# Five seven-product groups in every second gate-and-up block, gated results in DRAM, low parts on GpSimd

## The chip, the cores and the metric

The kernel runs on one core of a Trainium2 chip. The metric is device microseconds of one launch, the median of three timed runs. The engines are TensorE (PE in the profile; PEld is its weight load), VectorE (DVE), ScalarE (ACT), GpSimd (POOL) and SyncE (SP, which here only issues DMAs).

## The reference, cut to what matters

One decoder layer, 256 tokens, width 2048, all in float32: a first SwiGLU feed-forward network, a gated pair of token mixers (retention and sliding-window attention), a second SwiGLU network, and a gated input embedding, with a layer norm behind each.

```python
def swiglu(x, w_gu, w_down):
    g, u = jnp.split(x @ w_gu, 2, axis=-1)
    return (jax.nn.silu(g) * u) @ w_down

h = layer_norm(alpha * h + 0.5 * swiglu(h, w_ffn1_gu[i], w_ffn1_down[i]), ...)
mixed = (sigmoid(gate_r) * ret_branch + sigmoid(gate_a) * att_branch) @ w_mix_out[i]
h = layer_norm(alpha * h + mixed, ...)
h = layer_norm(alpha * h + 0.5 * swiglu(h, w_ffn2_gu[i], w_ffn2_down[i]), ...)
ple = jax.nn.sigmoid(h @ w_ple_gate[i]) * (p[i] @ w_ple_proj[i])
h = layer_norm(alpha * h + ple, ...)
```

`w_gu` is 2048 by 11264, `w_down` 5632 by 2048.

## The kernel before, in words

**Products.** A float32 product is made of three matmuls in the rounded type fp32r: the high part of each operand is a cast on ScalarE, the low part is VectorE's subtraction of the cast from the raw value, and TensorE adds high times high, high times low and low times high (`Sum.add`, L410 to L412). So each weight that arrives costs ScalarE a cast, VectorE a subtraction and TensorE its matmuls.

**Blocks and units.** The gate-and-up product of a feed-forward network ("f1", "f2") goes in 11 blocks (0 to 10), each of 512 gate and 512 up columns; a block walks through the 2048 rows in eight units of 256 rows and 1 MB of weights. A unit is of one of two kinds:

- A plain unit, "P" (class `Unit`): one cast of 128x2048 (tile `h...`), one subtraction of 128x2048 (tile `lo`, shown as `l...`), and 8 products, 24 matmuls of 128x512.
- A seven-product unit, "S" (class `Seven`): a 2x2 multiplication done with 7 products in place of 8, so 21 matmuls. VectorE makes four sums of the weights (tile `u`: 1024, 512 and 512 elements for each partition, L243, L247, L248), a low part of three weight blocks (`lb`, 1536, L253) and a low part of the sums (`lu`, 2048, L257); ScalarE casts the three blocks (`hb`) and the sums (`hu`, in two halves). The products `p1`, `p6`, `p7` and `q5` of all S units of a block are collected in four PSUM banks of their own (`f_gu7s` and the like for block 7), the others in the block's own four banks (`f1g`). In the last S unit of a block `p1` and `q5` come first, and `lu` is read by the sixth matmul.

An S unit also needs sums of the activations ("forms": `seven_forms`, four VectorE operations, a cast, a low part). They are made once for the units 0 to 3 in block 0 (tile `f1f`).

**A block's end.** After the last S unit `seven_common` copies `p1` to SBUF (ScalarE) and makes three VectorE sums out of PSUM into a tile `eve` (L499 to L501), which frees the four banks for the next block's `f1g`. After the last unit two more sums add the block's own banks (L831), ScalarE applies the silu, and VectorE multiplies (L836). TensorE transposes the result (`turned`, L789, eight 128x128 matmuls) in a later gap between two units, and ScalarE copies it to SBUF: tiles `f1a...`, 1 MB for two blocks, where they wait for the down product.

**The order.** ORDERS gives the units of each block: "PPSSPSSP" is units 4, 5, 0, 1, 6, 2, 3, 7, so four of eight are S. VectorE's order is set by two clocks that the program keeps while it is written out: `pump` hands VectorE weight work until its clock has come up to TensorE's, and `after` does so ahead of each sum from PSUM. SP loads the weights in the order of use, as far as the slots allow: SBUF holds 23 slots of 1 MB, and a call `weights(n)` says how many the weights may take. In the blocks 1 to 10 that number falls by one with every second block, as the `f1a` tiles fill up.

**Down product.** Two blocks over 44 row groups; `convert` makes the high and low part of the activations of a group (tiles `f1ac`), and the forms of four groups are made on the way (`sums`, `f1forms`). Between the two feed-forward networks stand the mixers, made of the same units. GpSimd does nothing after the constants are made.

## Time and profile before

| | |
|---|---|
| median of 3 runs | 2252.26 us (2251.83 to 2252.43) |
| the profiled execution | 2252.07 us, span 2250.2 us, 1.87 us around it |
| TensorE busy | 2242.8 us, 100% of the span, 10435 matmuls |
| VectorE busy | 2025.6 us, 90% |
| ScalarE busy | 1221.1 us, 54% |
| GpSimd busy | 0.7 us, 7 instructions |
| moved by DMA | 465.31 MB, 207 GB/s in the mean |

Gate-and-up blocks 2 to 10 of f1 follow each other every 41.69 us, the first of them from 91.41 us of the span. Numbers are lost in the profile's names: `lf_gu` is the low part of any P unit of such a block, `uf_gu`, `lbf_gu`, `luf_gu` are the tiles of any S unit. "Idle before" is the time that an engine stood still ahead of the instruction, and behind the arrow stands what ended it.

### The profile page before, as it was taken

To read this page: it belongs to the slowest core of one execution; us is meant where nothing else is said; L and a number is where in the kernel's file an instruction comes from. 1 tells how busy PE (TensorE), PEld (TensorE's weight loads), DVE (VectorE), ACT (ScalarE), POOL (GpSimd) and SP (SyncE) were. 2 spreads that over 40 slices of the span, in tenths; PEclk is the share of its full clock that TensorE was granted. 3 is DMA by queue.
4 is the path that set the end of the run, shared out by engine and by line. 5 is a ranking of instruction groups with operands and counts; after the bars stand their busy time and mean duration, and the time that the engine had idled before them with its cause. 6 is when DMAs were issued, how large, how long until landed. Compare 5 with 4: busy or idle time off the path is not lost.

```text
span 2250.2 us, 26572 instructions
## 1 busy us (share of the span) xinstructions
PE 2242.8 (100%) x10435; PEld 1870.6 (83%) x10435; DVE 2025.6 (90%) x1778; ACT 1221.1 (54%) x1030; POOL 0.7 (0%) x7
## 2 busy tenths in 40 slices
PE   9999999999999999999999999999999999999999
PEld 7888888888888888888888888888888888888887
DVE  7999999999997888899899878989999999989976
ACT  6655555555554455555555545455555566565542
POOL 0000000000000000000000000000000000000000
PEclk9999999999999999999999999999999999999999
DMA  8665665555577454355566665766566566555761
GB/s 318 206 214 179 214 206 186 190 204 206 210 271 264 166 221 150 137 197 193 168 210 220 195 215 195 271 230 216 174 206 213 185 201 207 187 213 214 281 268 70
DMA packets 189981, 465.31 MB, mean 207 GB/s; under 512 B 14368, under 2 KB 15904, under 8 KB 187296
## 3 DMA queue, kind: packets, MB, share of 16 engines
q1 hardware_dynamic: 188880, 462.43, 59.6%
q8 instruction: 82, 1.34, 0.2%
q10 hardware_dynamic: 976, 1.18, 0.2%
q14 instruction: 43, 0.35, 0.0%
HBM read 455.17 MB, written 8.39 MB: 206 GB/s over the span
## 4 chain that ended last, share of the span: by engine, by line
PE 99%; DMA 0%; DVE 0%; SPq 0%; ACT 0%; issue 0%; DVEq 0%; ACTq 0%
PE f1g L412 5%; PE f1g L410 5%; PE f1g L411 5%; PE f2g L411 4%; PE f2g L412 4%; PE f2g L410 4%; PE rqk L371 3%; PE aqk L371 2%; PE f2d L412 1%; PE f1d L411 1%; PE f2d L410 1%; PE f1d L410 1%; PE f1d L412 1%; PE f2d L411 1%; PE rqk L379 1%; PE f2e L412 1%
## 5 line engine op out<-in xcount | busy, mean ns | idle before, releaser
L208 DVE TENSOR_TENSOR lf_gu<-rf_gu,hf_gu 128x2048 fp32r<-128x2048 f32 x93 | 209.4, 2286 | 8.4 <-ACT hf_gu L204 8.4
L204 ACT CAST hf_gu<-rf_gu 128x2048 fp32r<-128x2048 f32 x93 | 175.9, 1909 | 34.4 <-DMA rf_gu<-in_f_gu 18.4
L257 DVE TENSOR_TENSOR luf_gu<-uf_gu,huf_gu 128x2048 fp32r<-128x2048 f32 x80 | 182.8, 2285 | 1.1 <-ACT huf_gu L249 1.1
L244 ACT CAST huf_gu<-uf_gu 128x1024 fp32r<-128x1024 f32 x80 | 84.2, 1053 | 141.8 <-DVE uf_gu L243 139.7
L412 PE MATMUL f1g<-lf_gu,xt 128*128 128x512 f32 x384 | 149.7, 390 | 0.5 <-DVE lf_gu L142 0.5
L410 PE MATMUL f1g<-hf_gu,xt 128*128 128x512 f32 x384 | 150.1, 391 | 0.1
L411 PE MATMUL f1g<-hf_gu,xt 128*128 128x512 f32 x384 | 149.7, 390 | 0.0
L208 DVE TENSOR_TENSOR lf_down<-rf_down,hf_down 128x2048 fp32r<-128x2048 f32 x60 | 136.2, 2287 | 13.5 <-ACT hf_down L204 5.5
L236 ACT CAST hbf_gu<-rf_gu 128x1536 fp32r<-128x1536 f32 x80 | 117.2, 1483 | 55.1 <-DMA rf_gu<-in_f_gu 40.2
L253 DVE TENSOR_TENSOR lbf_gu<-rf_gu,hbf_gu 128x1536 fp32r<-128x1536 f32 x80 | 140.1, 1751 | 0.0
L204 ACT CAST hf_down<-rf_down 128x2048 fp32r<-128x2048 f32 x60 | 114.3, 1913 | 47.5 <-DMA rf_down<-in_f_down 14.2
L410 PE MATMUL f2g<-hf_gu,ht 128*128 128x512 f32 x320 | 124.7, 390 | 0.0
L412 PE MATMUL f2g<-lf_gu,ht 128*128 128x512 f32 x320 | 124.7, 390 | 0.0
L411 PE MATMUL f2g<-hf_gu,ht 128*128 128x512 f32 x320 | 124.6, 390 | 0.0
L249 ACT CAST huf_gu<-uf_gu 128x1024 fp32r<-128x1024 f32 x80 | 84.2, 1052 | 34.2 <-DVE uf_gu L248 34.1
L243 DVE TENSOR_TENSOR uf_gu<-rf_gu 128x1024 f32<-128x1024 f32 x80 | 97.5, 1219 | 0.0
L412 PEld LDWEIGHTS f1g<-lf_gu,xt 128*128 128x128 f32 x384 | 72.1, 188 | 16.1 <-DVE lf_gu L142 1.2
L410 PEld LDWEIGHTS f1g<-hf_gu,xt 128*128 128x128 f32 x384 | 72.2, 188 | 15.3 <-ACT hf_gu L141 0.6
L411 PEld LDWEIGHTS f1g<-hf_gu,xt 128*128 128x128 f32 x384 | 72.3, 188 | 14.9
L257 DVE TENSOR_TENSOR luf_down<-uf_down,huf_down 128x2048 fp32r<-128x2048 f32 x28 | 64.0, 2287 | 7.8 <-ACT huf_down L249 5.9
L411 PEld LDWEIGHTS f2g<-hf_gu,ht 128*128 128x128 f32 x320 | 60.1, 188 | 12.4
L410 PEld LDWEIGHTS f2g<-hf_gu,ht 128*128 128x128 f32 x320 | 60.1, 188 | 12.4
(1331 smaller groups left out, 6418.6 us busy)
## 6 DMA issues: line engine op xcount, KB each, us to landing
rf_gu<-in_f_gu SPq DMA_DIRECT2D x350, 512.0 KB, 5.2
rf_down<-in_f_down SPq DMA_DIRECT2D x176, 512.0 KB, 4.5
rw_rv<-in_w_rv SPq DMA_DIRECT2D x32, 512.0 KB, 4.4
rrg<-in_w_in_f SPq DMA_DIRECT2D x32, 512.0 KB, 4.6
rgr<-in_w_in_f SPq DMA_DIRECT2D x32, 512.0 KB, 4.6
rw_ret<-in_w_ret SPq DMA_DIRECT2D x32, 512.0 KB, 5.0
rga<-in_w_in_f SPq DMA_DIRECT2D x32, 512.0 KB, 5.0
rw_mix<-in_w_mix SPq DMA_DIRECT2D x32, 512.0 KB, 4.5
```

Source lines behind the costliest of these rows:

```text
L204: act.copy(self.hi, self.raw)
L208: dve.tensor_tensor(self.lo, self.raw, self.hi, ALU.subtract)
L236: act.copy(quarters(self.hb), self.place.blocks(self.raw)[:, 1:])
L243: dve.tensor_tensor(at[:, 0:2], raw[:, 1:3], raw[:, 0:1].broadcast_to([P, 2, 2, 256]), ALU.add)
L244: act.copy(hu[:, 0:2], u[:, 0:2])
L249: act.copy(hu[:, 2:], u[:, 2:])
L253: dve.tensor_tensor(quarters(lb), raw[:, 1:], quarters(hb), ALU.subtract)
L257: dve.tensor_tensor(lu, u, hu, ALU.subtract)
L371: pe.matmul(ps[:, f], u.tile_of(kk)[0][:, f * P : (f + 1) * P], rhs(k), start=k == 0, stop=k == KD - 1,)
L410: pe.matmul(o, al, bh, start=first, stop=False)
L411: pe.matmul(o, ah, bh, start=False, stop=False)
L412: pe.matmul(o, ah, bl, start=False, stop=self.left == 0)
```

## The change

- Blocks 2, 4, 6 and 8 of both networks become "PSSPSSSP": units 5, 0, 1, 6, 2, 3, 4, 7 with five S. The fifth takes a second, smaller set of forms (`x4`), made in block 1 and held in a slot. In such a block no job is put between its units, so the transposes of the block before wait for the next block, which then has two sets.
- The gated results of two blocks are written to DRAM as soon as both are there (from ScalarE's queue, 1 MB, five times in a network), and are read back by SP (tiles `f1b...`) during the last block and the first down block. Weights may take 18 slots in all blocks from 1 on, 15 in the last.
- `help` gives GpSimd the low part of the next unit whose cast is there, two of its row groups (1024 elements) at a time, held back by a dependency until VectorE has ended what precedes the sums from PSUM. It stands ahead of L499 and ahead of the two L831 sums, and in the mixers' `joined`. VectorE then makes only the rest of that low part, and `lu` in two halves.
- The norm between mixers and f2 keeps one tile more, and has one slot less.

The core of the diff:

```diff
 ORDERS = {
     "f1": (
-        "PPPPPPPP", "PPSSPSSP", "PPSSPSSP", "PPSSPSSP", "PPSSPSSP", "PPSSPSSP", "PPSSPSSP", "PPSSPSSP", "PPSSPSSP",
-        "PPSSPSSP", "PPSSSPSP",
+        "PPPPPPPP", "PPSSPSSP", "PSSPSSSP", "PPSSPSSP", "PSSPSSSP", "PPSSPSSP", "PSSPSSSP", "PPSSPSSP",
+        "PSSPSSSP", "PPSSPSSP", "PPSSSPSP",
     ),
...
+        def help(self):
+
+            if not self.helped:
+                self.low()
+                room["used"] += 1
+            at = self.helped
+            self.helped = min(at + 2, self.low_rows)
+            return self.low_of(pool, slice(at, self.helped))
+
+        def low_rest(self):
+            if not self.helped:
+                self.low()
+            if self.helped < self.low_rows:
+                self.low_of(dve, slice(self.helped, self.low_rows))
+                spend(512 * (self.low_rows - self.helped))
...
-            dve.tensor_tensor(lu, u, hu, ALU.subtract)
-            spend(2048)
+            for at in (slice(0, 2), slice(2, 4)) if self.helped else (slice(0, 4),):
+                dve.tensor_tensor(lu[:, at], u[:, at], hu[:, at], ALU.subtract)
+                spend(512 * (at.stop - at.start))
...
+    def help():
+
+        u = loaded[0] if loaded else None
+        if u is None or not u.cast or isinstance(u, Columns) or u.helped == u.low_rows:
+            return
+        if not u.helped and room["slots"] <= room["used"]:
+            return
+        behind = mybir.DependencyInfo(mybir.DependencyClass.Sync, mybir.DependencyReason.DATA)
+        tc.add_manual_dep(ins_of(u.help()), ins_of(dve.done).name, behind, reason="beside reads of PSUM")
...
         after()
+        help()
         spend(512, 512, 1024)
         dve.tensor_tensor(e[:, 0], e[:, 1], p6, ALU.add)
...
+            if j % 2:
+                put[j // 2] = dram.tile([P, 8, S], F32, name=f"{name}p{j}")
+                act.dma_start(put[j // 2], raws.pop(j // 2))
+
+        put = {}
+
+        def fetch(q):
+
+            if q in put and q not in raws:
+                raws[q] = slot([P, 8, S], F32, f"{name}b{q}")
+                sync.dma_start(raws[q], put[q])
...
             if j:
-                weights(SLOTS - 5 - (j + 1) // 2 - (2 if j == KF // 4 - 1 else 0))
+                weights(SLOTS - 5 - (3 if j == KF // 4 - 1 else 0))
...
+                if j == 1 and u == 6:
+                    hl = slot([P, 2, 8, P], F32R, name + "f4")
+                    made["x4"] = seven_forms(keep()[1][:, :4], (hl[:, 0], hl[:, 1]))
...
                 v = got[0]
                 after()
+                help()
                 spend(1024, 1024)
```

VectorE at the end of block 1 and the start of block 2 of f1 (`lf_gu_5`: low part of P unit 5; `sums`, `f1f_667`: the second set of forms). Before:

```order
47 L208 TENSOR_TENSOR lf_gu_7_625<-rf_gu_7_509,hf_gu_7_583 128x2048
48 L208 TENSOR_TENSOR lf_gu_4_653<-rf_gu_4_578,hf_gu_4_623 128x2048
49 L208 TENSOR_TENSOR lf_gu_5_660<-rf_gu_5_592,hf_gu_5_651 128x2048
50 L243 TENSOR_TENSOR uf_gu_0_688<-rf_gu_0_627 128x1024
51 L247 TENSOR_TENSOR uf_gu_0_688<-rf_gu_0_627,uf_gu_0_688 128x512
52 L248 TENSOR_TENSOR uf_gu_0_688<-uf_gu_0_688,rf_gu_0_627 128x512
53 L253 TENSOR_TENSOR lbf_gu_0_695<-rf_gu_0_627,hbf_gu_0_658 128x1536
54 L499 TENSOR_TENSOR eve<-eve,f_gu1s_523 128x512
55 L500 TENSOR_TENSOR eve<-eve,f_gu1s_524 128x512
56 L501 TENSOR_TENSOR eve<-f_gu1s_524,eve 128x2x512
57 L257 TENSOR_TENSOR luf_gu_0_729<-uf_gu_0_688,huf_gu_0_689 128x2048
```

Ahead of the sums from PSUM stands one low part of a P unit less now, and the forms more. In the changed kernel all of VectorE's instructions carry the line L138:

```order
50 L138 TENSOR_TENSOR uf_gu_0_660<-uf_gu_0_660,rf_gu_0_592 128x512
51 L138 TENSOR_TENSOR sums<-xraw_177 128x256 x2
52 L138 TENSOR_TENSOR sums<-sums,xraw_177 128x256
53 L138 TENSOR_TENSOR sums<-xraw_177,sums 128x256
54 L138 TENSOR_TENSOR f1f_667<-sums,f1f_667 128x1024
55 L138 TENSOR_TENSOR lbf_gu_0_699<-rf_gu_0_592,hbf_gu_0_651 128x1536
56 L138 TENSOR_TENSOR eve<-eve,f_gu1s_523 128x512
57 L138 TENSOR_TENSOR eve<-eve,f_gu1s_524 128x512
58 L138 TENSOR_TENSOR eve<-f_gu1s_524,eve 128x2x512
59 L138 TENSOR_TENSOR luf_gu_0_732<-uf_gu_0_660,huf_gu_0_661 128x2048
```

The forms stand between the sums of unit 0 and its `lb`, ahead of the three `eve` operations. VectorE at the start of block 8 of f1, from the two sums of block 7's own banks (`eve<-eve,f1g`) on, in the changed kernel:

```order
248 L138 TENSOR_TENSOR eve<-eve,f1g_2251 128x1024
249 L138 TENSOR_TENSOR eve<-eve,f1g_2252 128x1024
250 L138 TENSOR_TENSOR luf_gu_0_2556<-uf_gu_0_2509,huf_gu_0_2510 128x2048
251 L138 TENSOR_TENSOR eve<-eve 128x2x512
252 L138 TENSOR_TENSOR uf_gu_1_2610<-rf_gu_1_2476 128x1024
253 L138 TENSOR_TENSOR uf_gu_1_2610<-rf_gu_1_2476,uf_gu_1_2610 128x512
254 L138 TENSOR_TENSOR uf_gu_1_2610<-uf_gu_1_2610,rf_gu_1_2476 128x512
255 L138 TENSOR_TENSOR luf_gu_1_2617<-uf_gu_1_2610,huf_gu_1_2611 128x1024 x2
256 L138 TENSOR_TENSOR lf_gu_6_2646<-rf_gu_6_2504,hf_gu_6_2608 128x2048
```

Here the `lb` of unit 1 is gone from VectorE's order; before, that place read:

```order
241 L243 TENSOR_TENSOR uf_gu_1_2565<-rf_gu_1_2454 128x1024
242 L247 TENSOR_TENSOR uf_gu_1_2565<-rf_gu_1_2454,uf_gu_1_2565 128x512
243 L248 TENSOR_TENSOR uf_gu_1_2565<-uf_gu_1_2565,rf_gu_1_2454 128x512
244 L253 TENSOR_TENSOR lbf_gu_1_2608<-rf_gu_1_2454,hbf_gu_1_2493 128x1536
245 L257 TENSOR_TENSOR luf_gu_1_2610<-uf_gu_1_2565,huf_gu_1_2566 128x2048
246 L208 TENSOR_TENSOR lf_gu_6_2635<-rf_gu_6_2461,hf_gu_6_2563 128x2048
```

From there the changed kernel goes on with the units 2, 3 and 4 whole (five VectorE operations each), then unit 7 of this block and units 4 and 5 of the next, and then block 8's `eve`. GpSimd's rows for blocks 8, 9 and 10 of f1 and the first down block (45 such rows in all, none before):

```order
22 L287 TENSOR_TENSOR lbf_gu_1_2518<-rf_gu_1_2476,hbf_gu_1_2507 128x1024
23 L287 TENSOR_TENSOR lbf_gu_1_2518<-rf_gu_1_2476,hbf_gu_1_2507 128x512
24 L287 TENSOR_TENSOR lbf_gu_0_2809<-rf_gu_0_2790,hbf_gu_0_2800 128x1024
25 L287 TENSOR_TENSOR lbf_gu_1_2847<-rf_gu_1_2797,hbf_gu_1_2838 128x1024
26 L287 TENSOR_TENSOR lbf_gu_0_3121<-rf_gu_0_3081,hbf_gu_0_3112 128x1024
27 L287 TENSOR_TENSOR lbf_gu_1_3162<-rf_gu_1_3109,hbf_gu_1_3150 128x1024
28 L233 TENSOR_TENSOR lf_down_1_3423<-rf_down_1_3352,hf_down_1_3414 128x1024
29 L233 TENSOR_TENSOR lf_down_3_3467<-rf_down_3_3418,hf_down_3_3460 128x1024
```

So a pair of blocks moves one whole `lb` and two thirds of two more from VectorE to GpSimd.

More of the change, by code (lines that the diff above doesn't have):

```diff
@@ L75 @@
 AHEAD = 5
+FETCH = 3
 MIXERS = {
@@ L236, in high, with low, low_of @@
             act.copy(quarters(self.hb), self.place.blocks(self.raw)[:, 1:])
+        def low(self):
+            self.lb = slot([P, 3, 512], F32R, "lb" + self.name)
+        def low_of(self, engine, at):
+            raw = self.place.blocks(self.raw)[:, 1:]
+            return engine.tensor_tensor(quarters(self.lb)[:, at], raw[:, at], quarters(self.hb)[:, at], ALU.subtract)
         def make(self):
@@ L276, in load @@
             first = loaded[0] if loaded else plan[0]
-            if plan[0].loads + first.makes - first.cast > room["slots"] - room["used"]:
+            if plan[0].loads + first.makes - first.early() > room["slots"] - room["used"]:
                 return
@@ L294, in step @@
         if not making:
-            if not loaded or loaded[0].makes - loaded[0].cast > room["slots"] - room["used"]:
+            if not loaded or loaded[0].makes - loaded[0].early() > room["slots"] - room["used"]:
                 return False
-            cast(loaded[0])
+            if not loaded[0].cast:
+                cast(loaded[0])
             u = loaded.pop(0)
-            room["used"] += u.makes - 1
+            room["used"] += u.makes - u.early()
             making.append((u, u.make()))
@@ L574, in __init__ @@
             self.i, self.eps, self.away = i, eps, away
-            self.keep = slot([P, 8, S], F32, f"keep{i}") if keep else None
+            self.keep = [slot([P, 8, S], F32, f"keep{i}{j}") for j in range(keep)]
             self.mvr = {}
@@ L601, in turn @@
             split(dst[:, :, t * P : (t + 1) * P], dst[:, :, S + t * P : S + (t + 1) * P], ps)
-            if self.keep is not None and k0 < 8:
-                act.copy(self.keep[:, k0 : k0 + nk, t * P : (t + 1) * P], ps)
+            if k0 // 8 < len(self.keep):
+                n = min(nk, 12 - k0)
+                act.copy(self.keep[k0 // 8][:, k0 % 8 : k0 % 8 + n, t * P : (t + 1) * P], ps[:, :n])
         def at(self, part, n):
@@ L870, in before_unit @@
         def before_unit(u):
+            for g in todo:
+                if firsts[groups.index(g)] <= u + AHEAD + FETCH:
+                    fetch(g // 2)
             while todo and firsts[groups.index(todo[0])] <= u + AHEAD:
@@ L877, in before_unit @@
                 convert(g)
-            left = {g // 2 for g in todo}
+            left = {g // 2 for g in todo if g // 2 in raws or g // 2 not in put}
             others(len(left) + len(groups) - len(todo) + 1 + (1 if u >= 10 else 0))
@@ L968, in joined @@
         after()
+        help()
         spend(1024, 1024)
```

62 lines of the change are left out of this document (41 added, 21 removed).

## The prediction

> **What bounds the kernel now.** I read the page first (busy times, the throttle's clock, the chain that ended last, the costliest groups), then stretches of time as long as a block, then the timelines of VectorE and TensorE where blocks meet.
>
> ```profile
> PE 2242.8 (100%) x10435; PEld 1870.6 (83%) x10435; DVE 2025.6 (90%) x1778; ACT 1221.1 (54%) x1030; POOL 0.7 (0%) x7
> PEclk9999999999999999999999999999999999999999
> PE 99%; DMA 0%; DVE 0%; SPq 0%; ACT 0%; issue 0%; DVEq 0%; ACTq 0%
> L412 PE MATMUL f1g<-lf_gu,xt 128*128 128x512 f32 x384 | 149.7, 390 | 0.5 <-DVE lf_gu L142 0.5
> rf_gu<-in_f_gu SPq DMA_DIRECT2D x350, 512.0 KB, 5.2
> 341.57:383.26 41.69, 41.69 (x190) 34.64 (x188) 40.27 (x31) 24.07 (x19) 0.00 (x0) 1.00 0.61 202
> ```
>
> TensorE is busy for the whole span at full clock and is 99% of the chain that ended last. The last row is one block (8 of f1): 41.69 us long, TensorE 41.69, VectorE 40.27, ScalarE 24.07, GpSimd nothing, clock 1.00, DMA share 0.61. So TensorE bounds, VectorE has 1.4 us left for each block, and fewer matmuls help only while VectorE keeps up.
>
> ```profile
> 341.34 0.39 PE L412 MATMUL f1g<-lf_gu,xt 128*128 128x512 f32 x1
> 341.57 0.39 PE L410 MATMUL f1g<-hf_gu,xt 128*128 128x512 f32 x1
> 341.79 0.39 PE L411 MATMUL f1g<-hf_gu,xt 128*128 128x512 f32 x1
> ```
>
> A matmul lasts 0.39 us but one starts every 0.227 us: P takes 24 x 0.2267 = 5.44 us, S 21 x 0.2267 = 4.76 us. Block 8 starts at T = 341.57. VectorE around it:
>
> ```profile
> 336.18 0.68 DVE L499 TENSOR_TENSOR eve<-eve,f_gu7s 128x512 f32<-128x512 f32 x1
> 337.69 1.22 DVE L501 TENSOR_TENSOR eve<-f_gu7s,eve 128x1024 f32<-128x1024 f32 x1
> 338.83 1.22 DVE L243 TENSOR_TENSOR uf_gu<-rf_gu 128x1024 f32<-128x1024 f32 x1
> 341.09 2.35 DVE L831 TENSOR_TENSOR eve<-eve,f1g 128x1024 f32<-128x1024 f32 x2 [1.04 <-PE f1g L412]
> 343.36 0.68 DVE L247 TENSOR_TENSOR uf_gu<-rf_gu,uf_gu 128x512 f32<-128x512 f32 x1
> 344.68 1.22 DVE L836 TENSOR_TENSOR eve<-eve 128x1024 f32<-128x1024 f32 x1
> 345.82 1.75 DVE L253 TENSOR_TENSOR lbf_gu<-rf_gu,hbf_gu 128x1536 fp32r<-128x1536 f32 x1
> 347.49 2.29 DVE L257 TENSOR_TENSOR luf_gu<-uf_gu,huf_gu 128x2048 fp32r<-128x2048 f32 x1
> 349.69 1.22 DVE L243 TENSOR_TENSOR uf_gu<-rf_gu 128x1024 f32<-128x1024 f32 x1
> 356.14 2.29 DVE L208 TENSOR_TENSOR lf_gu<-rf_gu,hf_gu 128x2048 fp32r<-128x2048 f32 x1
> 358.35 1.22 DVE L243 TENSOR_TENSOR uf_gu<-rf_gu 128x1024 f32<-128x1024 f32 x1
> ```
>
> From start to start: `lb` 1.67, `lu` 2.20, a P unit 2.21, a whole S unit 6.45 (349.69 to 356.14), so its three sums 6.45 - 1.67 - 2.20 = 2.58; the multiplication 1.14; the three `eve` sums 2.65; the two L831 sums 2.27, ended at T + 1.79. VectorE's one wait is the 1.04 us for the block's last matmuls.
>
> **The change part by part.** *Matmuls:* eight blocks give up one P for one S: 8 x 3 = 24 matmuls, 24 x 0.2267 = 5.44 us, 0.68 for each block. That is all the change can gain.
>
> *A five-S block in the steady state (4, 6, 8 of both networks).* On TensorE two P and four S stand ahead of the last S: 2 x 5.44 + 4 x 4.76 = 29.92; it reads `lu` at its sixth matmul, 1.13 later: T + 31.05. VectorE leaves the L831 sums at T + 1.79 as now (the four-S block ahead gives it room to wait there), then `lu` of unit 0 2.20, the multiplication 1.14, the sums of unit 1 2.58 (its `lb` is GpSimd's), its `lu` in two halves 2.27 (as the two L831), unit 6 2.21, units 2, 3 and 4 3 x 6.45 = 19.35: 31.54, and the last operation ends 0.09 behind its pitch (2.29 against 2.20): T + 31.63. So TensorE waits 0.6 us there, and the 0.68 saved is nearly gone: -0.1 a block, -0.5 for six. The bounds: -0.68 (VectorE somehow 0.6 earlier) and +0.6 (it leaves the sums 0.7 later); the sum is taken from the rows. Over the pair VectorE suffices: one S for P is 6.45 - 2.21 = 4.24 more, the help is 1.67 + 2 x 1.13 = 3.9 less, halving costs about 0.2, so 0.5 of the present 2 x 1.4 goes. It is the place in the block that is wrong, not the total.
>
> *Block 2 of f1.* VectorE has no room in block 1:
>
> ```profile
> 78.05 6.69 DVE L208 TENSOR_TENSOR lf_gu<-rf_gu,hf_gu 128x2048 fp32r<-128x2048 f32 x3
> 88.93 0.69 DVE L499 TENSOR_TENSOR eve<-eve,f_gu1s 128x512 f32<-128x512 f32 x1
> 90.44 1.22 DVE L501 TENSOR_TENSOR eve<-f_gu1s,eve 128x1024 f32<-128x1024 f32 x1
> 91.58 2.28 DVE L257 TENSOR_TENSOR luf_gu<-uf_gu,huf_gu 128x2048 fp32r<-128x2048 f32 x1
> 92.09 0.39 PE L410 MATMUL f1g<-hf_gu,xt 128*128 128x512 f32 x1
> 516.71 0.42 DVE L481 TENSOR_TENSOR sums<-f1a 128x256 f32<-128x256 f32 x1
> 519.37 1.23 DVE L142 TENSOR_TENSOR f1forms<-sums,f1forms 128x1024 fp32r<-128x1024 f32 x1 [1.11 <-ACT f1forms L141]
> 520.51 1.22 DVE L142 TENSOR_TENSOR f1ac<-f1a,f1ac 128x1024 fp32r<-128x1024 f32 x1
> ```
>
> No wait stands in these rows. `eve` is done at 90.44 + 1.22 = 91.66, just ahead of TensorE's use of the second pair of those banks at 92.09 (block 2 starts at 91.41). The change takes one of the three low parts of P units away (-2.20) and puts the forms in; a set of that size lasts 520.51 - 516.71 = 3.80 in the down product, wait for the cast included. `eve` is done 1.6 later, at 93.26: TensorE stands 1.17. Then VectorE goes on at 93.18: 2.20, the L831 sums 2.26, 2.58, 1.14, 2.27, 2.21 and 19.35 end at 125.28; TensorE wants the last `lu` at 91.41 + 1.17 + 31.05 = 123.63 and stands 1.65 more. 2.82 - 0.68 = +2.1 (-0.7 if the forms fit into waits I do not see, +2.8 if the cast is late).
>
> *Block 2 of f2.*
>
> ```profile
> 1536.99 0.69 DVE L499 TENSOR_TENSOR eve<-eve,f_gu1s 128x512 f32<-128x512 f32 x1 [0.85 <-ACT eve L496]
> 1538.51 1.22 DVE L501 TENSOR_TENSOR eve<-f_gu1s,eve 128x1024 f32<-128x1024 f32 x1
> ```
>
> Here VectorE waits 0.85, and `eve` ends over 2 us before block 2 starts (1541.95): 1.6 more is covered. -0.7.
>
> *GpSimd's operations.* No trace row has one of this kind. The nearest are VectorE's 1.22 for 1024 elements and GpSimd's own longest:
>
> ```profile
> 1.04 0.29 POOL masks.py:199 TENSOR_SCALAR_AFFINE_SELECT ident<-ident 128x128 f32<-128x128 f32 x1
> ```
>
> Eight such for 1024 elements make 2.3 at most, if all of it goes by elements. Between 1.2 and 2.3 it fits beside the `eve` sums (2.65) or the L831 pair (2.27, with the 1.04 of waiting ahead). The parts are read late: unit 1's `lb` when TensorE comes to that unit, T + 5.44 + 4.76 = 10.2. I cost it at nothing; if the cover goes, see the second rival. The Trainium skill (GPSIMD Engine Reference, section "Elementwise — side-by-side cycle accounting") gives 4497 ns for 2048 elements against VectorE's 2293; by it 1024 would take about 2.25 us, an estimate, and the sum would be the same.
>
> *Put and fetch.* Ten writes and ten reads of 1 MB, 21 of 465 MB. A load of 512 KB lands in 5.2 us at a DMA share of 0.61; a 1 MB put every 83 us is hidden. ScalarE gets 1.7 a block more of casts, from 24.07 of 41.69: hidden. The fetches stand in SP's one queue ahead of weight loads, and wait for slots there, so in the down product casts and low parts come later:
>
> ```profile
> 505.65 2.29 DVE L208 TENSOR_TENSOR lf_down<-rf_down,hf_down 128x2048 fp32r<-128x2048 f32 x1 [0.29 <-issue]
> 530.17 2.29 DVE L208 TENSOR_TENSOR lf_down<-rf_down,hf_down 128x2048 fp32r<-128x2048 f32 x1 [0.84 <-ACT hf_down L204]
> 541.58 2.29 DVE L257 TENSOR_TENSOR luf_down<-uf_down,huf_down 128x2048 fp32r<-128x2048 f32 x1
> 544.15 0.39 PE L412 MATMUL f_down0s<-luf_down,f1forms 128*128 128x512 f32 x1
> ```
>
> The last two rows are the fifth S unit of the first down block: `lu` is ready at 543.87, read at 544.15, with 0.28 to spare. In the new order the forms and low parts ahead of it wait for slots that TensorE frees about a unit later. The waits of 0.29 and 0.84 there are the nearest: one or both once more costs TensorE 0.0 to 0.9 in each network. I take 0.5 each, +1.0, with 0 and +1.8 as ends. The putting by itself opens a slot or more to the weights in the blocks; no row shows TensorE waiting for loads, so nothing is gained.
>
> *Mixers and norm:* five low parts leave VectorE, a copy comes to ScalarE (54% busy). Nothing, since TensorE does not wait there now.
>
> **The sum:** -0.5 + 2.1 - 0.7 + 1.0 = +1.9 on the profiled 2252.07 (span 2250.2 and 1.87 around it), 2254.0; the median stands 0.19 above that execution: 2254.2, no change that can be told (0.2%, 4.5 us, is about what a measurement here can tell).
>
> **The rivals.** *VectorE keeps up* (faster): if the help puts it some 0.7 us further ahead in each block (the sums are left earlier than T + 1.79, or S units run closer than 6.45), only block 2 of f1 costs: 2252.26 - 5.44 to 2252.26 - 3, so 2246.8 to 2249. For it speaks that VectorE's total suffices; against it that the L831 sums cannot start before TensorE ends the block, and that all ten operations behind them are counted at pitches that repeat to 0.01. Faster than 0.2% needs more than 4.5 of the 5.44.
>
> *GpSimd and VectorE keep each other out* (slower): should a GpSimd subtraction and a VectorE operation not run at once, VectorE stands still for the 3.9 a pair at its own pace, or for twice that at 2.3 for 1024 elements. The pair has 2 x 1.4 - 0.5 = 2.3 to spare: 1.6 to 5.5 is over, in 8 pairs 13 to 44, so 2265 to 2296. It passes 0.2% when more than 2.3 + 0.3 = 2.6 of a pair's 3.9 is not hidden (2.3 us over the forecast, spread over 8 pairs). The Trainium skill (SBUF — State Buffer, section "SBUF: two separate sides") says that the two share a port pair as an exclusive lock, against VectorE operations with two inputs in SBUF; by this rule the sums from PSUM would be free of it, and what runs over into the next unit's sums would block. No row of this trace shows it, since GpSimd makes nothing there yet.
>
> *The fetches stall the down product* (slower): each fetch waits in SP's queue for a slot with the weights behind it. If each of the ten costs 0.5 to 1, 5 to 10 us in place of my 1.0: 2258 to 2263. Against it: ScalarE and VectorE still wait little for loads there.
>
> *The change does nothing:* excluded for the matmuls, whose count falls; GpSimd's rows are in the order.
>
> **How the numbers follow.** Forecast (net -4.5 to +4.5 by small stalls) 0.60, VectorE keeps up to more than 0.2% 0.19, GpSimd excluded 0.08, fetches or like stalls beyond 0.2% 0.13. The ends of my terms give 2252.26 - 4.1 - 0.7 - 0.7 = 2246.8 and 2252.26 + 3.6 + 2.8 - 0.7 + 1.8 = 2259.8; not all fall on one side at once, so the low end is 2247.0, and the slower rivals pull the high one to 2261.0.
>
> **What would show it.** 24 matmuls less; five-S blocks of about 40.7 us with a wait of about 0.6 ahead of the last S's `lu` products, ended by `luf_gu`; waits of 1.2 and 1.7 in block 2 of f1; GpSimd operations of 1.2 to 2.3 us with VectorE's sums at their old 0.69 and 1.22 beside them; small waits at the fifth S of the first down block. I am wrong if VectorE's operations grow beside GpSimd's, if no wait stands at the last S, or if TensorE waits for weights.

## The result, and the profile after

Slower: 2266.46 us (median of 4 runs, 2265.56 to 2268.11) against 2252.06 (median of 4); the ratio is 1.0065, 95% interval 1.0047 to 1.0082. The forecast was 2254.2 (2247.0 to 2261.0): no change. The profiled execution took 2267.16 us, its span 2265.4.

From the page (busy time of each engine with its number of instructions; the chain that ended last; GpSimd's costliest group):

```profile
PE 2243.5 (99%) x10411; PEld 1865.7 (82%) x10411; DVE 2025.2 (89%) x1843; ACT 1236.8 (55%) x1050; POOL 100.2 (4%) x52
PE 85%; DVE 8%; issue 1%; ACT 1%; DMA 1%; DVEq 0%; SPq 0%; ACTq 0%
L287 POOL TENSOR_TENSOR lbf_gu<-rf_gu,hbf_gu 128x1024 fp32r<-128x1024 f32 (+1 forms) x36 | 77.8, 2161 | 808.7 <-DVE lf_gu L138 295.7
```

The 24 matmuls are gone (10435 to 10411), but TensorE's share of the chain fell from 99% to 85% and VectorE's rose to 8%: TensorE now waits. For what, the view of its waits says (engine, tile and line; what it waited for: total us, times, longest):

```profile
PE f_down0s L476 <- DVE lbf_down L138: 5.8, 2, 2.9
PE f_gu8s L476 <- DVE luf_gu L138: 1.8, 2, 0.9
PE f_gu6s L476 <- DVE luf_gu L138: 1.7, 2, 0.8
PE f_gu4s L476 <- DVE luf_gu L138: 1.6, 2, 0.8
PE f_gu2s L476 <- DVE luf_gu L138: 1.2, 1, 1.2
PE f1g L474 <- DVE eve L138: 1.2, 1, 1.2
```

The places are those that the forecast named: the last S unit of the five-S blocks, block 2 of f1, one S unit of the first down block (`f_down0s`). That unit is the fourth of the block's six S units; the prediction and the expectations call it the fifth. The sizes are not those of the forecast. The table gives, for the profiled execution of this kernel and of those below, by how much TensorE's lead over the kernel before changed in each stretch: the start of its first matmul on a weight unit, less the same start before; plus is time lost. A five-S block is taken together with the block behind it, to which the change moves transposes.

| kernel | f1 block 2 | f1 blocks 4, 6, 8 | f1 first down block | mixers, f2 blocks 0 and 1 | f2 block 2 | f2 blocks 4, 6, 8 | f2 first down block |
|---|---|---|---|---|---|---|---|
| forecast | +2.1 | -0.3 | +0.5 | 0 | -0.7 | -0.3 | +0.5 |
| after | +2.78 | +1.43 | +4.79 | +0.53 | -0.68 | +1.44 | +3.34 |
| e1_no_put | +2.61 | +1.38 | 0 | +0.22 | -0.68 | +1.35 | 0 |
| e2_put_only | +0.16 | 0 | +5.85 | +0.01 | 0 | 0 | +4.59 |
| e9_four2 | +0.86 | -0.08 | +6.02 | +1.51 | -0.68 | +1.45 | +4.80 |
| e10_copy_first | +2.71 | +3.11 | +4.80 | +1.42 | -0.68 | +3.11 | +3.35 |
| e12_two_pairs | +2.80 | +1.42 | 0 | +0.54 | -0.68 | +1.40 | 0 |
| e14_hold | +2.26 | +0.54 | +4.76 | +1.24 | -0.68 | +0.54 | +3.32 |
| e15_hold_low | +2.63 | -2.04 | +4.77 | +0.61 | -0.67 | -2.05 | +4.80 |
| e16_hold_all | +1.40 | -1.49 | 0 | +0.04 | -0.68 | -1.47 | 0 |

After: 13.6 us of the 15.2 that the span grew. The other 1.6 lie behind the last matmul: the last output writes are issued 4.7 us before the span's end, before it was 3.0. That differs between executions, whatever the kernel (0 in the profiled one of e2, 1.6 in that of e12).

*The first down block* is the largest loss. ScalarE's casts of three P units, then TensorE at the fourth S unit, by their timelines (start, duration, what, and in brackets the idle time ahead and who ended it):

```profile
509.74 1.91 ACT L225 CAST hf_down<-rf_down 128x2048 fp32r<-128x2048 f32 x1 [0.90 <-PE f1d L475]
519.94 1.91 ACT L225 CAST hf_down<-rf_down 128x2048 fp32r<-128x2048 f32 x1 [2.29 <-PE f1d L475]
535.81 1.92 ACT L225 CAST hf_down<-rf_down 128x2048 fp32r<-128x2048 f32 x1 [2.07 <-PE f1d L476]
549.30 0.50 PE L476 MATMUL f_down0s<-lbf_down,f1ac 128*128 128x512 f32 x1 [2.88 <-DVE lbf_down L138]
550.51 0.63 PE L474 MATMUL f1d<-hbf_down,f1forms 128*128 128x512 f32 x1
```

The casts wait not for their weights (landed 10 to 16 us earlier) but for TensorE: each starts about when TensorE leaves a unit. VectorE's low parts come behind them, and TensorE stands 2.88 us for the `lb` of the fourth S unit. Then the matmuls themselves are long (0.63 us instead of 0.39). Stretches of time behind the idle time (last three columns: clock granted, DMA share, GB/s), the last row from the same place of f2:

```profile
549.24:550.30 1.06, 1.00 (x4) 0.87 (x5) 1.06 (x2) 1.06 (x1) 0.00 (x0) 0.91 0.36 35
550.30:553.70 3.40, 3.40 (x9) 2.63 (x9) 3.40 (x3) 2.38 (x3) 0.00 (x0) 0.53 0.81 304
553.70:556.00 2.30, 2.30 (x11) 1.88 (x11) 2.30 (x2) 2.02 (x2) 0.00 (x0) 1.00 0.00 0
2005.90:2009.50 3.60, 3.57 (x15) 2.76 (x16) 3.60 (x2) 2.59 (x2) 0.00 (x0) 1.00 0.65 215
```

Behind the idle time the granted clock is 0.53 in the mean for 3.4 us: 4.79 us lost by an idle time of 2.88. In f2 TensorE stands for the same 2.88 us, but the clock stays at 1.00, and 3.34 us are lost. So about 1.45 of f1's 4.79 us go with the clock.

*Blocks 4, 6 and 8.* Block 8 of f1 starts at T = 345.16 here. VectorE around it, ScalarE's two rows ahead of it, and VectorE's last `lu` and TensorE at the last S unit, from their timelines:

```profile
336.51 1.22 DVE L138 TENSOR_TENSOR uf_gu<-rf_gu 128x1024 f32<-128x1024 f32 x1
339.38 1.48 DVE L138 TENSOR_TENSOR eve<-eve,f_gu7s 128x512 f32<-128x512 f32 x2 [1.65 <-ACT eve L560]
342.04 0.68 DVE L138 TENSOR_TENSOR uf_gu<-rf_gu,uf_gu 128x512 f32<-128x512 f32 x1
343.36 1.75 DVE L138 TENSOR_TENSOR lbf_gu<-rf_gu,hbf_gu 128x1536 fp32r<-128x1536 f32 x1
345.03 2.34 DVE L138 TENSOR_TENSOR eve<-eve,f1g 128x1024 f32<-128x1024 f32 x2
347.30 2.28 DVE L138 TENSOR_TENSOR luf_gu<-uf_gu,huf_gu 128x2048 fp32r<-128x2048 f32 x1
337.82 1.06 ACT L295 CAST huf_gu<-uf_gu 128x1024 fp32r<-128x1024 f32 x1 [3.84 <-DVE uf_gu L138]
338.78 0.57 ACT L560 COPY eve<-f_gu7s 128x512 f32<-128x512 f32 x1
374.94 2.28 DVE L138 TENSOR_TENSOR luf_gu<-uf_gu,huf_gu 128x2048 fp32r<-128x2048 f32 x1
377.28 0.50 PE L476 MATMUL f_gu8s<-luf_gu,f1f 128*128 128x512 f32 x1 [0.91 <-DVE luf_gu L138]
```

VectorE stands idle 1.65 us ahead of the `eve` sums, for ScalarE's copy of p1 (L560). That copy stands in ScalarE's queue behind a cast that waits for VectorE's own `uf_gu`. Between `eve` and the sums from PSUM now lie the rest of `u` and `lb` (342.04 to 345.03, 2.99 us), where before lay 1.14 and a wait of 1.04. So the sums start without a wait, and VectorE leaves them at 347.30, T + 2.14.

### The profile page after: what moved, and what is told of

The parts are those of the page before. It is cut to its first block, busy times and chain, and to the rows that moved or that the text cites. A ratio compares the mean times of both kernels' runs of the same rounds, so it can differ in the third digit from the quotient of the medians.

```text
span 2265.4 us, 26852 instructions
## 1 busy us (share of the span) xinstructions
PE 2243.5 (99%) x10411; PEld 1865.7 (82%) x10411; DVE 2025.2 (89%) x1843; ACT 1236.8 (55%) x1050; POOL 100.2 (4%) x52
## 4 chain that ended last, share of the span: by engine, by line
PE 85%; DVE 8%; issue 1%; ACT 1%; DMA 1%; DVEq 0%; SPq 0%; ACTq 0%
PE f2g L476 4%; PE f2g L474 4%; PE f2g L475 4%; PE rqk L435 3%; PE f1g L476 3%; PE f1g L475 3%; PE f1g L474 3%; DVE luf_gu L138 3%; DVE uf_gu L138 2%; PE aqk L435 2%; DVE lbf_gu L138 1%; PE rqk L443 1%; PE f1d L476 1%; PE f2e L475 1%; PE f2e L474 1%; PE f1e L475 1%
## 5 line engine op out<-in xcount | busy, mean ns | idle before, releaser
L138 DVE TENSOR_TENSOR lf_gu<-rf_gu,hf_gu 128x2048 fp32r<-128x2048 f32 (+2 forms) x93 | 199.2, 2170 | 16.6 <-ACT hf_gu L225 13.3
L138 DVE TENSOR_TENSOR luf_gu<-uf_gu,huf_gu 128x2048 fp32r<-128x2048 f32 (+1 forms) x116 | 203.4, 1770 | 3.6 <-ACT huf_gu L300 3.3
L295 ACT CAST huf_gu<-uf_gu 128x1024 fp32r<-128x1024 f32 x88 | 92.6, 1053 | 193.3 <-DVE uf_gu L138 193.3
L225 ACT CAST hf_gu<-rf_gu 128x2048 fp32r<-128x2048 f32 x85 | 160.8, 1908 | 31.7 <-DMA rf_gu<-in_f_gu 18.9
L138 DVE TENSOR_TENSOR lf_down<-rf_down,hf_down 128x2048 fp32r<-128x2048 f32 (+1 forms) x60 | 132.0, 2216 | 27.5 <-ACT hf_down L225 15.3
L474 PE MATMUL f1g<-hf_gu,xt 128*128 128x512 f32 x352 | 138.1, 392 | 1.2 <-DVE eve L138 1.2
L475 PE MATMUL f1g<-hf_gu,xt 128*128 128x512 f32 x352 | 137.5, 390 | 0.0
L300 ACT CAST huf_gu<-uf_gu 128x1024 fp32r<-128x1024 f32 x88 | 92.7, 1054 | 53.4 <-DVE uf_gu L138 53.3
L138 DVE TENSOR_TENSOR lbf_gu<-rf_gu,hbf_gu 128x1536 fp32r<-128x1536 f32 (+1 forms) x80 | 118.8, 1485 | 0.0
L287 POOL TENSOR_TENSOR lbf_gu<-rf_gu,hbf_gu 128x1024 fp32r<-128x1024 f32 (+1 forms) x36 | 77.8, 2161 | 808.7 <-DVE lf_gu L138 295.7
L474 PE MATMUL f2g<-hf_gu,ht 128*128 128x512 f32 x288 | 112.4, 390 | 0.0
L475 PE MATMUL f2g<-hf_gu,ht 128*128 128x512 f32 x288 | 112.1, 389 | 0.0
L138 DVE TENSOR_TENSOR uf_gu<-rf_gu 128x1024 f32<-128x1024 f32 x88 | 107.1, 1217 | 0.3 <-PE f2t L855 0.3
L138 DVE TENSOR_TENSOR luf_down<-uf_down,huf_down 128x2048 fp32r<-128x2048 f32 x28 | 64.0, 2286 | 5.6 <-ACT huf_down L300 5.4
L138 DVE TENSOR_TENSOR uf_gu<-rf_gu,uf_gu 128x512 f32<-128x512 f32 x88 | 63.6, 723 | 2.5
```

What stands on the lines that cost most here:

```text
L138: self.done = call(*a, **k)
L225: act.copy(self.hi, self.raw)
L287: return engine.tensor_tensor(quarters(self.lb)[:, at], raw[:, at], quarters(self.hb)[:, at], ALU.subtract)
L295: act.copy(hu[:, 0:2], u[:, 0:2])
L300: act.copy(hu[:, 2:], u[:, 2:])
L474: pe.matmul(o, al, bh, start=first, stop=False)
```

## The experiments

**Which part costs what.** First the parts alone. In e1 the gated results stay in SBUF, and the blocks, the forms and GpSimd's help are as changed, and the weights have the slots of before, less one for the second forms:

```
-            if j % 2:
-                put[j // 2] = dram.tile([P, 8, S], F32, name=f"{name}p{j}")
-                act.dma_start(put[j // 2], raws.pop(j // 2))
...
-                weights(SLOTS - 5 - (3 if j == KF // 4 - 1 else 0))
+                weights(SLOTS - 5 - (j + 1) // 2 - (2 if j == KF // 4 - 1 else 1 if j < 9 else 0))
```

> Five-S blocks, second forms and GpSimd's parts stay; the gated results stay in SBUF as before (no put, no fetch; the weights get the slots of before, less one for the second forms). Theory A (the waits of 4.8 and 3.3 us at the fifth S unit of the first down block come from putting and fetching): they are gone, 2266.5 - 8.1 = 2258.3. Rival B (they come from GpSimd's parts in the first down block, which change VectorE's order): they stay, about 2266.

Measured: 2257.64 (2257.28 to 2259.11), ratio 1.0026 [1.0015, 1.0036]. The table's two columns of the down block are 0; the rest stays. e2 is the reverse, the kernel before with put and fetch alone (four S units in every block, no GpSimd, one set of kept forms).

> The kernel before with put and fetch alone (four S everywhere, no GpSimd, no second forms). Theory A: the down blocks lose 4.8 and 3.3 us here too, and nothing else changes: 2252.1 + 8.1 = 2260.2. Rival B: 2252. If moving 20 MB more costs time by itself, a loss spread over the blocks.

Measured: 2259.78 (2258.56 to 2262.73), 1.0035 [1.0021, 1.0049]. Nearly all of its loss is the down block's, +5.85 and +4.59. The profiled execution took 2262.53 us, 2.75 more than the median. TensorE's row there, from its timeline:

```profile
544.84 0.79 PE L476 MATMUL f_down0s<-lbf_down,f1ac 128*128 128x512 f32 x1 [2.70 <-DVE lbf_down L138]
```

The 5 us behind it as a stretch of time (the count behind TensorE's busy time is that of its matmuls; the clock is third from the end):

```profile
545.00:550.00 5.00, 5.00 (x12) 3.94 (x13) 5.00 (x3) 3.97 (x3) 0.00 (x0) 0.50 0.73 263
```

The same stretch of the kernel before:

```profile
545.00:550.00 5.00, 5.00 (x23) 4.15 (x23) 4.36 (x3) 3.03 (x3) 0.00 (x0) 1.00 1.03 402
```

A shorter idle time (2.70), but half the clock for 5 us behind it: 12 matmuls instead of 23. What follows from the two runs: put and fetch cost some 8 us (8.1 by the table's row of the change, 8.8 by e1's median, 7.6 by e2's), all in the first down blocks, and without GpSimd's help as well as with it. The rest of the loss is there without any put.

In e3 GpSimd makes no low parts (`help` does nothing).

> The changed kernel with all low parts back on VectorE (GpSimd makes none). Theory E (GpSimd's help is worth what VectorE no longer does, and its operations cost VectorE almost nothing): 3.9 us of VectorE's work come back in each of 8 pairs of blocks, of which about 1.6 us of its idle time in front of the sums out of PSUM can take a part; in each five-S block the last S comes later by at least the 1.7 us of the lb: 2266.5 + 8 x 1.7 to 8 x 3.9, 2280 to 2298. Rival F (GpSimd and VectorE keep each other out, so the help is worth nothing): about 2266, or faster.

Measured: 2290.92 (2289.15 to 2291.65), 1.0172 [1.0155, 1.0189]: GpSimd's help is worth 24.5 us, inside theory E's range, and rival F falls. Without the help TensorE waits for VectorE two or three times in a five-S block:

```profile
PE f_gu6s L476 <- DVE lbf_gu L138: 4.0, 4, 1.2
PE f_gu6s L476 <- DVE luf_gu L138: 2.5, 2, 1.2
PE f_gu8s L476 <- DVE lbf_gu L138: 2.2, 2, 1.1
```

Part of this loss goes with the clock. In block 6 of f1 two of the waits, 1.25 and 1.24 us, end 2.2 us apart (at 299.22 and 301.42), and behind the second the clock is at half for some 3 us:

```profile
301.90:305.00 3.10, 3.10 (x9) 2.45 (x8) 3.10 (x2) 3.10 (x4) 0.00 (x0) 0.50 0.68 200
```

So it is in three of the seven blocks of e3 that have such a pair of waits.

**The down block.** Two runs gave the weights less room, by the theory that with the fetches more slots are promised than there are. e6 counts the pairs that are not yet fetched as well; e7 also keeps block 10 to 11 slots:

```
-            left = {g // 2 for g in todo if g // 2 in raws or g // 2 not in put}
+            left = {g // 2 for g in todo}
```

> The changed kernel, but in the first down block a gated result that is not yet fetched is counted as holding its slot, as before the change, so that the weights leave the slot free. Theory A1 (the fetched tiles find the slots taken by weights that were let in too early; fetches, casts and forms then wait for TensorE to release slots): the down loss is gone, 2258.3. Rival A2 (the fetches are late or hold up SP whatever the slots): it stays, 2266.

> As e6_room (unfetched results counted as holding a slot), and in block 10 the weights may take 11 slots as before the change, not 15, so that the slots are free from the start of the down product. Theory A1 (too many slots held by weights when the fetches come): the loss at the fifth S unit of the first down block is gone in both networks, 2258.3. Rival A2 (the fetches themselves are late in SP's queue or take a slot for too long): it stays, 2266.

Measured: 2267.04 (2265.33 to 2269.48) and 2267.45 (2266.25 to 2268.16), 1.0067 [1.0052, 1.0082] and 1.0066 [1.0051, 1.0081]. No change; the theory falls. The next one: slots are handed out in the order in which they came free in the program, and the fetched pairs shift that order, so that casts get slots that TensorE has not left. e12 puts by only the first two pairs, which are fetched in block 10, and gives the weights fewer slots to match (that line is left out here):

```
-            if j % 2:
+            if j % 2 and j // 2 < 2:
```

> Only the first two pairs of gated results of each network are put by and fetched; the other three stay in SBUF as in the kernel before. Theory R (slots are handed out in the order in which they were released; with the fetched pairs the casts in the first down block get slots that TensorE has not yet left, and wait one unit for it): the three pairs restore the order that the kernel without put had, and the loss at the fifth S unit of the first down block, 4.8 and 3.3 us, goes: 2258.4 (2257.0 to 2260.5). Rival (the transfers themselves are late or in the way of the weights): two fifths of the loss stay at least, 2261.5 to 2263.5. Rival (the first two fetches, in block 10, are what counts): no change, 2266.5.

Measured: 2257.35 (2256.99 to 2259.24), 1.0025 [1.0015, 1.0035]. The loss is gone in both networks, while two fifths of the transfers remain; what is gone are the fetches inside the down block, and their puts. The three casts again, in e12:

```profile
505.65 1.91 ACT L225 CAST hf_down<-rf_down 128x2048 fp32r<-128x2048 f32 x1
516.25 1.92 ACT L225 CAST hf_down<-rf_down 128x2048 fp32r<-128x2048 f32 x1 [0.61 <-DVE lbf_down L138]
532.24 1.91 ACT L225 CAST hf_down<-rf_down 128x2048 fp32r<-128x2048 f32 x1 [1.14 <-DVE luf_down L138]
```

They start 4.1, 3.7 and 3.6 us earlier, and none of the three waits for TensorE. Shown: the loss comes with the pairs that are fetched inside the down block, and in the changed kernel it goes through casts that wait for TensorE. In e2, which loses at the same matmul, it is partly VectorE that waits:

```profile
505.46 4.49 DVE L138 TENSOR_TENSOR lf_down<-rf_down,hf_down 128x2048 fp32r<-128x2048 f32 x2 [1.94 <-PE f1d L475]
```

Both fit the theory that tiles get slots that TensorE still holds, but that is an argument from the order of the program: no run changed the order of slots alone.

**The last S unit of the five-S blocks.** e5 gives it the ordinary order of products, in which `lu` is read two products later but p1, p6 and p7 are ready later:

```
-            if p == sevens[-1]:
+            if p == sevens[-1] and len(set(p for k, p in units if k == "S")) != 5:
```

> The changed kernel, but in the five-S blocks the last S unit takes its products in the ordinary order, so that its lu is read at the twelfth matmul and not the sixth (1.36 us later). Theory C (each steady five-S block waits 1.1 to 1.2 us for that lu and for nothing else): the six steady blocks give 6 x 1.15 and block 2 of f1 about 1.4: 2266.5 - 8.3 = 2258.2. Rival D (the sums out of PSUM then come later and TensorE waits for the banks in the next block): no gain, 2266 or more.

Measured: 2264.23 (2263.68 to 2267.1), 1.0057 [1.0042, 1.0072]; 2.2 us gained of the 8.3 expected, with intervals that overlap those of the change. The waits for `lu` went, others came:

```profile
PE f1g L474 <- DVE eve L138: 3.6, 5, 1.2
PE f2g L474 <- DVE eve L138: 1.4, 3, 0.6
```

The next block's first matmuls now wait for `eve`: the rival that the expectation named took most of it. e8 attacks VectorE's order instead: in blocks 3, 5 and 7 more of the next unit's `u` goes ahead of `eve`, and its `lu` ahead of the sums.

```
-        pump(clock["pe"] - 15 * MATMUL)
+        pump(clock["pe"] - clock["lead"] * MATMUL)      # lead is -6 in blocks 3, 5, 7
...
-                after()
+                after(clock["pe"] + (2.0 if j in (3, 5, 7) else 0))
```

> The changed kernel, but at the end of the blocks 3, 5 and 7 VectorE makes the second step of the sums of the next block's unit 0 ahead of the three eve sums (where it now stands idle 1.65 us) and its lu ahead of the two sums of the block's own banks. Theory G (in the five-S block VectorE is late because it idles before eve and then has 5.65 us to do in the 5.44 us up to the block's end): the last S's lu is ready about 1.3 us earlier, the six waits of 1.1 us go, 2266.5 - 6.6 = 2259.9. Rival H (VectorE's whole work in a five-S block is too much, as e5_last_order hinted, and the wait only moves to the next bank use): 2264 or more.

Measured: 2268.03 (2266.59 to 2268.24), 1.0068 [1.0053, 1.0083]. No gain. The row shows why: `eve` still waits, only later.

```profile
340.79 1.48 DVE L138 TENSOR_TENSOR eve<-eve,f_gu7s 128x512 f32<-128x512 f32 x2 [1.60 <-ACT eve L560]
```

In both orders ScalarE's copy stands behind a cast that waits for VectorE. So e10 issues the copy ahead of all casts of the next unit, and e11 adds the `lu` ahead of the sums:

```
-        pump(clock["pe"] - 15 * MATMUL)
-        if not EARLY_COPY:
+        if clock["early"]:                              # in the blocks ahead of the five-S ones
             act.copy(e[:, 1], p1)
+        pump(clock["pe"] - (0 if clock["early"] else 15) * MATMUL)
```

> One order is changed in gate and up blocks 2, 4, 6 and 8: ScalarE's copy of the product p1 (L560) is issued ahead of the casts of the next block's first S unit, behind which it stood. Theory H (the copy waits in ScalarE's queue behind a cast that waits for VectorE, so VectorE stands idle 1.65 us ahead of the eve sums): that idle goes, the sums from PSUM start when TensorE ends the block (T - 0.48 instead of T - 0.13), and the wait for the last low part of the fifth S unit shrinks by the same 0.35 us, from 1.6 to 1.8 to about 1.3 a pair of blocks: 6 x 0.35 = 2.1 us, 2264.4 (2263.4 to 2265.4). Rival (VectorE has simply more work than time, in whatever order): no change, 2266.5. Rival (the copy now holds the casts behind it until p1 is complete): slower, 2267 to 2270.

> As the run with the copy first, and in blocks 4, 6 and 8 VectorE also makes the next block's first lu (2.35 us) ahead of its sums from PSUM instead of behind them. Theory H: with the copy out of the way the idle 1.65 us and the 0.35 us before the sums hold most of that lu, so the work behind the sums ends some 1.5 us sooner, and the wait at the fifth S unit (1.1 us of TensorE time a block) goes: 6 x 1.1 = 6.6 us, 2259.9 (2258.5 to 2262.0). Rival (VectorE has more work than time): 2266.5. The run in which the same lu went ahead without the copy being moved gained nothing, 2268.0.

Measured: 2270.5 (2269.53 to 2275.84), 1.009 [1.0073, 1.0107], and 2272.94 (2269.95 to 2275.53), 1.0092 [1.0077, 1.0108]: both slower. In e10, ScalarE, GpSimd and VectorE:

```profile
338.18 0.59 ACT L560 COPY eve<-f_gu7s 128x512 f32<-128x512 f32 x1 [6.06 <-PE f_gu7s L476]
338.67 2.86 ACT L280 CAST hbf_gu<-rf_gu 128x1536 fp32r<-128x1536 f32 x2
338.81 1.48 DVE L138 TENSOR_TENSOR eve<-eve,f_gu7s 128x512 f32<-128x512 f32 x2 [0.17 <-ACT eve L560]
341.60 2.80 POOL L287 TENSOR_TENSOR lbf_gu<-rf_gu,hbf_gu 128x1024 fp32r<-128x1024 f32 x1 [34.37 <-DVE eve L138]
342.18 2.77 DVE L138 TENSOR_TENSOR uf_gu<-uf_gu,rf_gu 128x512 f32<-128x512 f32 x1
```

VectorE's idle time is 0.17 instead of 1.65, as expected. But two casts of `hb` now stand behind the copy, which itself waits 6.06 us for TensorE. GpSimd needs `hb`, which ends at 338.67 + 2.86 = 341.53 (the view names `eve`, which ends within 0.02 us of it). So it starts 4.54 us ahead of block 8 (341.60, the block at 346.14) instead of 7.30 (337.86 and 345.16 in the changed kernel), no longer beside the sums from PSUM but beside a VectorE sum of two SBUF inputs, and that one takes 2.77 us instead of 0.69. I had not thought of those casts.

e14 holds back only the one cast that waits for VectorE; `hb` stays ahead of the copy. e15 is e14 with the `lu` ahead of the sums:

```
-            act.copy(hu[:, 0:2], u[:, 0:2])
+            held_back.append(lambda: act.copy(hu[:, 0:2], u[:, 0:2]))
+            if not clock["copy first"]:
+                held_back.pop()()
...
+        if first:
             act.copy(e[:, 1], p1)
+            while held_back:
+                held_back.pop(0)()
```

> In gate and up blocks 2, 4, 6 and 8 the copy of p1 stands ahead of one cast alone, that of the next block's first u, which waits for VectorE; the casts of hb, which GpSimd's low parts need, stay ahead of the copy. No other engine's order changes. Theory H (ScalarE's queue makes VectorE idle; the two runs before lost again because the hb casts came late, so that GpSimd's 2.4 us ran into VectorE's sums of two SBUF inputs, 2.77 us instead of 0.69): idle 1.65 gone, sums from PSUM 0.35 us sooner, six times: 2264.4 (2263.4 to 2265.4). Rival (VectorE has more work than time in whatever order): 2266.5. If the collision with GpSimd was not what the two runs lost: 2269 to 2271 again.

> As the run with the one cast held, and the first lu of blocks 4, 6 and 8 (and of block 2 of the second network) goes ahead of the sums from PSUM. Theory H: it lands in the idle that the copy leaves, the low parts behind the sums are ready 1.4 us sooner, the wait at the fifth S unit (1.1 us of TensorE time a block) goes: 2266.5 - 6.6 = 2259.9 (2258.5 to 2262.0). Rival (more work than time): 2266.5.

Measured: 2266.03 (2264.45 to 2269.29), 1.0067 [1.0052, 1.0082], and 2260.01 (2259.4 to 2261.62), 1.0036 [1.0023, 1.005]. In e14, whose block 8 starts at T = 344.66:

```profile
336.70 0.59 ACT L564 COPY eve<-f_gu7s 128x512 f32<-128x512 f32 x1 [3.30 <-PE f_gu7s L479]
337.28 2.42 POOL L287 TENSOR_TENSOR lbf_gu<-rf_gu,hbf_gu 128x1024 fp32r<-128x1024 f32 x1 [31.53 <-ACT eve L564]
337.32 1.48 DVE L138 TENSOR_TENSOR eve<-eve,f_gu7s 128x512 f32<-128x512 f32 x2 [0.17 <-ACT eve L564]
344.18 2.35 DVE L138 TENSOR_TENSOR eve<-eve,f1g 128x1024 f32<-128x1024 f32 x2 [1.13 <-PE f1g L479]
```

GpSimd runs beside the `eve` sums again, and the sums of the block's own banks wait 1.13 us for TensorE, the idle time that the forecast had assumed to be there. The loss of a five-S block falls from 0.48 to 0.18 us (the table's 1.43 and 0.54 over three blocks); the median moved only 0.4 of the expected 2.1 us, and the intervals of the two kernels overlap, so by its time alone e14 decides nothing. In e15 the `lu` uses that idle time, the waits for `luf_gu` in blocks 4, 6 and 8 leave the view of waits, and each of these blocks gains its 0.68 us whole (-2.04 and -2.05 over three): 6.4 us faster than the change, its time the expected one to 0.1. The theory of ScalarE's queue stands, and VectorE has time enough. It takes both edits: the copy alone gave 0.3 us a block (e14), VectorE's new order alone none (e8).

**Block 2 of f1.** e9 leaves it four S units and makes the forms in it, not in block 1:

```
-        "PPPPPPPP", "PPSSPSSP", "PSSPSSSP", "PPSSPSSP", ...
+        "PPPPPPPP", "PPSSPSSP", "PPSSPSSP", "PPSSPSSP", ...
...
-                if j == 1 and u == 6:
+                if j == (1 if norm is not None else 2) and u == 6:
```

> The changed kernel, but block 2 of f1 keeps four S, and the second set of forms is made in block 2 and not in block 1. Theory I (block 2 of f1 costs 2.7 us because VectorE has no idle time in block 1 for 3.8 us of forms; a block later GpSimd's parts have made room): that is gone, 2266.5 - 2.7 = 2263.8. Rival J (the forms cost the same wherever they stand, and block 4 is late instead): 2266 or more.

Measured: 2263.02 (2261.45 to 2266.65), 1.005 [1.0035, 1.0065]; this interval overlaps that of the change, so the table decides. Block 2 costs 0.86 instead of 2.78; and block 4 of f1, with this change alone, gains its 0.68 too, which I had not expected.

**Together.** e13 is e1 with e9 and e11, e16 is e1 with e9 and e15:

> The parts that the runs so far point to in one kernel: gated results stay in SBUF, block 2 of the first network keeps four S units, the five-S blocks, the forms and GpSimd's low parts stay, the copy of p1 is first in ScalarE's queue and the first lu of the next block ahead of the sums. By theory H: 2257.6 of the kernel without put, less 3.2 for block 2, less 6.6 for the fifth S units: 2247.8 (2246.5 to 2250.5), faster than the kernel before by 0.2%. By the rival that VectorE has more work than time: 2254.4.

> As the run with the first lu ahead of the sums, and the gated results stay in SBUF, and block 2 of the first network keeps four S units. By theory H: 2257.6 of the kernel without put, less 3.2 for block 2, less 6.6 for six fifth S units: 2247.8 (2246.5 to 2250.5), faster than before by 0.2%. By the rival that VectorE has more work than time: 2254.4.

Measured: 2257.98 (2257.75 to 2259.92), 1.0028 [1.0017, 1.0038], and 2250.59 (2250.27 to 2251.79, 11 runs), 0.9994 [0.9985, 1.0003]. The first came out 10 us above its expectation; TensorE waits 1.24 us for `luf_gu` in five of its five-S blocks, as in e10. The second came out 2.8 us above its expectation, just beyond the upper end of 2250.5: block 2 of f1 still costs 1.40, and block 8 gains only 0.1 of its 0.68 in each network. It is the best of all kernels here, 1.5 us under the kernel before, which cannot be told from no change. What TensorE still waits for in e16's blocks:

```profile
PE f1g L477 <- DVE eve L138: 1.1, 1, 1.1
PE f_gu8s L479 <- DVE luf_gu L138: 0.5, 2, 0.3
```

## Why the prediction was wrong

The forecast missed by 12.3 us. Put and fetch make 7.1 of it, the six steady five-S blocks about 3.4. The first alone takes the time out of the range: its term had the ends 0 and +1.8 and measured 8.1.

*The matmuls* (5.44 us less, 0.68 a block): right. Wherever the waits were taken away, a block gains 0.68 (e15; block 2 of f2 everywhere).

*The steady five-S block* (-0.1 forecast, +0.48 measured): the step of this part that failed is "VectorE leaves the L831 sums at T + 1.79 as now (the four-S block ahead gives it room to wait there)". It left them at T + 2.14: the order puts 2.99 us between `eve` and the sums instead of 1.14, and `eve` could not start earlier, for the copy behind ScalarE's cast. I had followed VectorE's queue alone. The rest of that sum held: the last `lu` was forecast 29.84 behind the sums and came 29.92 behind them (374.94 + 2.28 = 377.22). What a late `lu` costs was undersized too: TensorE starts again 0.06 behind it, at 377.28, with a first matmul of 0.50, and the unit lasts 6.00 instead of 4.76, 1.24 us for a wait that the view counts as 0.91. The measured +0.48 lies inside the bounds of this part (-0.68 to +0.6).

*Block 2 of f1* (+2.1, measured +2.78): right in place and kind, both waits stand there, 1.18 and 1.24 us; the forecast was 1.17 and 1.65. The waits are shorter than forecast and the loss is larger, so a wait costs TensorE more than its idle time here too. The upper bound of +2.8 just holds. *Block 2 of f2* (-0.7, measured -0.68): right.

*GpSimd* (1.2 to 2.3 us for 1024 elements, hidden): the operation takes 2.41, just above the range. It is hidden on TensorE's path, and the sums from PSUM beside it keep their time (1.48 for two, 1.22 above). The rival that the two keep each other out is not what made the change slow (without GpSimd e3 is 24.5 us slower still), but half of its mechanism is real. In a four-S block GpSimd runs over into the next unit's sums:

```profile
388.27 2.41 POOL L287 TENSOR_TENSOR lbf_gu<-rf_gu,hbf_gu 128x1024 fp32r<-128x1024 f32 x1 [1.89 <-DVE uf_gu L138]
387.53 2.34 DVE L138 TENSOR_TENSOR eve<-eve,f1g 128x1024 f32<-128x1024 f32 x2
389.79 1.44 DVE L138 TENSOR_TENSOR uf_gu<-rf_gu,uf_gu 128x512 f32<-128x512 f32 x1
```

The sums from PSUM are not slowed; `uf_gu`, with two inputs in SBUF, takes 1.44 instead of 0.69, until GpSimd ends at 390.68. The Trainium skill (SBUF — State Buffer, section "SBUF: two separate sides") has this rule, an exclusive lock between GpSimd and VectorE operations with two SBUF inputs; the trace agrees.

*Put and fetch* (+0.5 in each network, measured +4.79 and +3.34): the mis-sized term, 7.1 us of the 12.3 by which the forecast missed. The place was right, and so, as far as the runs show it, was the chain (casts that wait for TensorE, then a late low part at that S unit; `lb` and not `lu` ends the wait). The size was not: "one or both once more costs TensorE 0.0 to 0.9" took the waits of before, 0.29 and 0.84, for the size of new ones, but a cast that waits for TensorE to leave a unit waits for what is left of a unit of 4.76 or 5.44 us (0.90, 2.29 and 2.07 here). The granted clock that falls behind the idle time was not in the forecast at all; it makes about 1.45 us of the 4.79. The rival "the fetches stall the down product" (5 to 10 us in place of 1.0, at a chance of 0.13) was the nearest to what happened, 8.1, but by its number alone: it had weights waiting in SP's queue, and the weights of the late casts had landed 10 to 16 us before.

Not explained: 0.0 to 1.5 us between the networks (1.8 in e11), in part at a wait for `eve` in the attention's projections that comes and goes between these kernels; and why e9's block 4 needed no further help.

## What to carry to other kernels

When work is moved in one engine's queue, follow each value that the moved work needs back through the other engines' queues: here a copy of 0.57 us stood behind a cast that waited for VectorE, and VectorE waited for the copy. An engine that is idle half of the time can still be late, if its next instruction waits. When tiles are added to a shared pool of slots, look at which later instructions start to wait for the slowest engine: three casts did here, and that it was for their slots is the likeliest reading, not a shown one. And a wait on an engine that runs at its limit costs more than its length (1.24 us for 0.91), and more again when the clock falls behind it.
